# One kernel, three edits: the last head group's values computed features by tokens and mixed two units to a bank, two output tiles by halves, and products exchanged at both ends of the down product

## The chip, the cores and the metric

The kernel runs on one core of a Trainium2 chip. The metric is the device time of one launch in microseconds; of several launches the median is taken. The profile is that of one execution.

## What is computed

Two layers over x of 1024 tokens by 1024 features, in float32. Each layer does this (cut from the reference):

```
hn = rmsnorm(h, norm1[i]);  z = hn @ w_in[i]
u = z[..., :256];  q, k, v = split(z[..., 256:], 3)          # 12 heads of 64
pool_out = pool_mixer(u, pool_w[i], pool_scale[i])
attn_out = dilated_mixer(rotary(q), rotary(k), v)            # 3 groups of 4 heads: (128,1) (512,4) (2048,16)
h = h + concatenate([pool_out, attn_out]) @ w_out[i]
h = h + square(relu(rmsnorm(h, norm2[i]) @ w_up[i])) @ w_down[i]
gate = sigmoid(rmsnorm(h, norm3[i]) @ w_gate[i])
h = h + gate * (p[i] @ w_ple[i])
```

A group's output is weighted per token and head by a softmax over the three groups' denominators, which is known only when all three groups have their scores.

## The kernel before

Activations stand features by tokens, 128 features to a tile, 1024 tokens in two halves of 512. A float32 product is made of three fp32r matmuls (high by high, high by low, low by high); `split` makes the high part on ScalarE and the low part on VectorE. `Weights.next()` hands out a group of weight columns, waits on the program's clock until its high and low parts have been issued, and begins the next group 0.6 us later, with 0.9 us from one step to the next.

Nothing is scheduled by the compiler: instructions go out in the order in which the program issues them, engine by engine. That order comes from a clock `ck` of the program's own. `ck.tick(ns)` advances it for each matmul and runs the generators that have come due; a generator issues some instructions and yields the delay to its next step; `ck.need(key)` runs queued events, and moves the clock on to them, until the key has been issued; some helpers add to `ck.now` for the matmuls that they issue themselves. So delays in the code are a plan, not waits: on the chip, engines wait for each other by semaphores, in the order issued.

In a layer the input product runs group by group: q, k, v of the first two groups, q and k of the third, the two tiles `us` of the pooling columns, and last the third group's values. For those, hT is the stationary operand: eight tiles v2p of 128 tokens by 256 features, 24 matmuls of 256 columns each; ScalarE scales them by the norm into v2. As each tile is ready, `alone(u)` mixes one unit of 128 tokens: four small matmuls into bank o (eight records in the trace), two ScalarE copies into oT. In the same stretch the pooling mixer ends (`mixed`: py on VectorE from sums pa and pb on GpSimd, then two matmuls pm for each tile, L944, split by L536 and L538), `joint` makes the softmax weights (jt, jw, a round trip through DRAM, wb), and `weigh` multiplies o by wb (L1026) and splits it into cat (L532, L534). Pooling's second tile begins T_M1 = 13.0 us, on the program's clock, after the last pooling product.

The output product follows: for m in 0 to 5 one weight group, two halves po, evicted by `out_evac`; the last two tiles are done together.

Up and down products use seven products instead of eight per 2x2 block (P1 to P7, in the Strassen manner). `Set.open` gives P1, P6, P5 and P3 of a set one bank X, P2 a bank Y, P7 and P4 a bank Z. A bank is read out after each product (in the down product by VectorE into acc, L1294), and the next product of the same bank adds to what is there, so it waits until that read is done. `Seven` makes the weight pieces (d0p, d1p) ahead of the products by planned times; `D7.lead` starts its plan before the down product begins. `x_back` loads the pieces wP of the squared activations that `Up.sums` wrote to DRAM. For the last two up sets (`rush`) these sums wait 33 us.

PSUM has 8 banks: mm 3, s 2, e 2, o 1.

Of the kernel before, what the change touches and what calls it, by code (L numbers as in the profile page):

```python
# [117 lines left out]
def body(nc, tc, pools, A, out):  # L118
# [3 lines left out]
    def blk(name, dt=F32, shape=(128, 1024)):  # L122
        return sb.tile(list(shape), dt, name=name, tag="b")

    def bank(name, tag, shape=(128, 512)):
        return ps.tile(list(shape), F32, name=name, tag=tag)
# [4 lines left out]
    def hs(hf):  # L131
        return slice(hf * 512, hf * 512 + 512)
# [207 lines left out]
    for L in range(DEPTH):  # L340
        wi, wo, wu, wd, wg = (A[n][L] for n in ("w_in", "w_out", "w_up", "w_down", "w_gate"))
        g1 = G_N1 + 8 * L

        def col(part, g):
            return POOLW + 768 * part + 256 * g

        for g in range(NPAT):
            for part in range(2 if g == 2 else 3):
                for m in range(2):
                    groups.append([(wi, 0, 8, col(part, g) + 128 * m, 128, g1)])  # L350
        for m in range(2):
            groups.append([(wi, 0, 8, 128 * m, 128, g1)])
        groups.append([(wi, 4 * a, 4, col(2, 2), 256, g1) for a in range(2)])
        for m in range(8):
            groups.append([(wo, 0, 8, 128 * m, 128, None)])
        sevens.append(([(wu, 0, 4, 256 * j) for j in range(FF // 256)],
                       [(wd, a, n, 256 * t) for t, a, n in STEPS]))
        dn0.append(len(groups))
        for rep in range(2 if L == DEPTH - 1 else 1):
            for m in range(8):  # L360
                groups.append([(wg, 0, 8, m * 128, 128, None)])
            for m in range(2):
                pgroups.append([(A["w_ple"][L], 0, 2, m * 512, 512, None)])
# [177 lines left out]
    def pair(name):  # L541
        return blk(name + "H", F32R), blk(name + "L", F32R)
# [80 lines left out]
    def layer(L, hT, norm, tabs):  # L623
# [97 lines left out]
        vdone = set()  # L721

        def vok(g, n, p):
            return ((2, n) if g == 2 else (g, p, n // 4)) in vdone

        def in_v(g):
            vs = []
# [127 lines left out]
        def attend(g, q, k, vget, base, gap, late):  # L855

            o = [blk(f"o{g}{p}_{L}") for p in range(2)]
            oT[g] = o
            units = [Unit(g, n, q, k, vget, o) for n in range(8)]

            def alone(u):
                yield 1500.0
                while not vok(g, u.n, 0):
                    yield 500.0
                u.mix()

            def beats():
                t = ck.now
                for i in range(8 + 2 * late):
                    if 0 <= i - late < 8:  # L870
                        u = units[i - late]
                        u.turn()
                        if g == 2:
                            ck.go(alone(u))
                    if g < 2 and i >= 2 * late:
                        u = units[i - 2 * late]
                        while not (vok(g, u.n, 0) and vok(g, u.n, 1)):
                            yield 500.0
                        u.mix()
                    if i < 8:  # L880
                        units[i].scores()
                    t += gap
                    yield max(100.0, t - ck.now)
            ck.go(beats(), delay=base)

        for g in range(2):
            q = in_qk(f"q{g}", g)
# [3 lines left out]
                   5000.0, 5900.0, 1)  # L891
        q = in_qk("q2", 2)
        k = in_qk("k2", 2)
        v2 = [blk(f"v2{a}_{L}", F32, (128, 4, 256)) for a in range(2)]
        attend(2, q, k, lambda n, h: v2[n // 4][:, n % 4, 64 * h:64 * h + 64],
               3500.0, 2500.0, 2)


        us = [blk(f"u{m}_{L}") for m in range(2)]
# [143 lines left out]
        for i in range(4):  # L1043
            cat[2 + i] = pair(f"cat{2 + i}_{L}")
            for hf in range(2):
                ck.go(weigh(i // 2, i % 2, hf), (id(cat[2 + i][0]), hf), W_0 + W_1 * (2 * i + hf))
        for t in range(8):
            p = bank(f"v2p{L}", "mm", (128, 256))
            tc_ = slice(t * 128, t * 128 + 128)
            for kk in range(8):  # L1050
                h, l = hT[kk]
                wh, wl = (x[:, kk % 4] for x in w[kk // 4])
                nc.tensor.matmul(p, h[:, tc_], wh, start=kk == 0, stop=False)
                nc.tensor.matmul(p, l[:, tc_], wh, start=False, stop=False)
                nc.tensor.matmul(p, h[:, tc_], wl, start=False, stop=kk == 7)
                if kk < 7:
                    ck.tick(330.0)
            nc.scalar.activation(v2[t // 4][:, t % 4], p, AF.Copy, scale=norm.rt[:, t:t + 1])
            ck.at(600.0, lambda t=t: vdone.add((2, t)))
            ck.tick(330.0)  # L1060
            if t in (3, 7):
                for i in (4, 5):
                    if t == 3:
                        cat[2 + i] = pair(f"cat{2 + i}_{L}")
                    hf = t // 7
                    ck.go(weigh(2, i % 2, hf), (id(cat[2 + i][0]), hf), 2500.0 + 900.0 * (i - 4))


        norm2 = Norm(f"b{L}")
# [95 lines left out]
        S7 = Seven(sevens[L][0], seq, f"u{L}", side=4)  # L1165

        catl = [cat[i] for i in range(8)]
        for m in range(6):
            w = W.next()
            if m == 5:  # L1170
                W.begin(W.i + 1, delay=5000.0)
            for hf in range(2):
                p = bank(f"po{L}", "mm")
                products(p, wk(w, range(8)), catl, hs(hf))
                ck.go(out_evac(p, m, hf))
# [29 lines left out]
        class Up(Set):  # L1205
# [34 lines left out]
            def sums(self, y):  # L1240
# [5 lines left out]
                nc.sync.dma_start(out=d[:, 0], in_=y[:, :512])  # L1246
                rush = self.j >= n7 - 2
                if rush:
                    yield 33000.0
                sub = nc.vector.tensor_tensor  # L1250
                slow = 1500.0 if rush else 700.0
                b11, b12, b21, b22 = y[:, :512], y[:, 512:], self.y2[:, :512], self.y2[:, 512:]
# [59 lines left out]
        seq2 = [(0, P) for P in RING[:6]]  # L1312
        for k in range(1, nst - 2):
            seq2 += [(k, "P1"), (k - 1, "P3")] + [(k, P) for P in RING[1:6]]
        seq2 += [(nst - 3, "P3")]
        seq2 += [(k, P) for P in ORDER for k in (nst - 2, nst - 1)]
        D7 = Seven(sevens[L][1], seq2, f"d{L}", (9, 6, 3))

        def run(S, seq, qs, objs, xs_of):
# [3 lines left out]
            for (j, P), o in zip(seq[qs[0]:], outs):  # L1323
                objs[j].close(o[0], P)

        live = {j: Up(j) for j in range(n7)}
        run(S7, seq, range(4), live, lambda j: xs)
        run(S7, seq, range(4, 6), live, lambda j: xs)
        for q in range(6, len(seq)):
            run(S7, seq, [q], live, lambda j: xs)  # L1330
            if q == len(seq) - 5:
                acc_load(0)
            if q == len(seq) - 8:
                D7.lead(8 * 12 * 225.0)
            n = q - len(seq) + 15
            if n > 0 and n % 2 == 0:
                for i in range(4):
                    ck.at(1500.0 * i + 300.0 * n, lambda i=i, P=seq[q][1]: ck.go(x_back(i, P)))


        live = {k: Down(k) for k in range(nst)}
        for q, (k, P) in enumerate(seq2):
            t, a, n = STEPS[k]
            if P == "P4" and k < 3:
# [1 line left out]
            if P == "P1":  # L1346
                if k >= nst - 2 and norm3 is None:
                    norm3 = Norm(f"c{L}")
            run(D7, seq2, [q], live, lambda k: xw[a:a + n])
            if t % 2 and k < nst - 2:  # L1350
                ck.go(x_back(a + 4, P))
                ck.at(5000.0, lambda i=a + 5, P=P: ck.go(x_back(i, P)))
# [236 lines left out]
```

## Time and profile before

| | |
|---|---|
| median of 3 runs | 2268.42 us (2268.37 to 2268.53) |
| profiled execution | 2269.02 us, span 2267.2 us, mean granted TensorE clock 0.999 |
| TensorE matmuls | 2240.3 us busy, 99% of the span |
| VectorE, ScalarE, GpSimd | 72%, 45%, 14% |

A span runs from the first to the last instruction. Matmuls overlap in the records, so what one costs is read from start to start, not from its duration. An idle time is put to the engine and instruction whose end came last before the waiting instruction began.

### The profile page before, as it was taken

What the parts mean: (1) busy time and instruction counts of PE and PEld (TensorE: products, weight loads), DVE (VectorE), ACT (ScalarE), POOL (GpSimd) and SP (SyncE); (2) the same over time, 40 slices, a digit from 0 to 9 for tenths busy, and PEclk for the clock granted to TensorE, in tenths of its full rate; (3) what the DMA queues carried; (4) which work ended last, traced back from release to release, by engine and by line L of the source; (5) the groups of instructions that cost most, each with busy time, mean ns of one, the idle gap of its engine ahead of it and who ended that gap; (6) DMA issues with size and microseconds to landing.
All of it is one profiled execution on the core that took longest, in us unless ns stands there. A gap on an engine that the chain in (4) does not pass through costs nothing.

```text
span 2267.2 us, 30544 instructions
## 1 busy us (share of the span) xinstructions
PE 2240.3 (99%) x11088; PEld 1849.0 (82%) x11088; DVE 1643.2 (72%) x3046; ACT 1011.6 (45%) x2147; POOL 313.9 (14%) x282
## 2 busy tenths in 40 slices
PE   8999999999999999999999999999999999999998
PEld 6887788888887888878887878888888878888888
DVE  6565757877778888796565567687777798888845
ACT  6244533533335434364324355444333453434645
POOL 5121135100000000022121122330000000000322
PEclk9999999999999999999999999999999999999999
DMA  6011133354448745431220122234445675546224
GB/s 186 19 48 20 39 94 112 124 167 150 150 143 271 239 135 171 149 112 47 61 62 19 39 49 61 81 112 153 153 154 160 209 247 175 162 140 181 69 62 134
DMA packets 296367, 275.63 MB, mean 122 GB/s; under 512 B 12476, under 2 KB 224056, under 8 KB 296216
## 3 DMA queue, kind: packets, MB, share of 16 engines
q1 hardware_dynamic: 293624, 270.04, 38.6%
q0 software_dynamic: 2272, 3.61, 0.9%
q8 instruction: 87, 1.43, 0.3%
q14 instruction: 64, 0.52, 0.1%
q10 hardware_dynamic: 320, 0.03, 0.0%
HBM read 200.99 MB, written 72.58 MB: 121 GB/s over the span
## 4 chain that ended last, share of the span: by engine, by line
PE 91%; DVE 5%; DMA 1%; ACT 1%; issue 1%; POOL 1%; SPq 0%; DVEq 0%; ACTq 0%
PE X L567 29%; PE Z L567 14%; PE Y L567 7%; PE in L552 5%; PE in L554 5%; PE in L550 5%; PE gt L554 3%; PE gt L552 3%; PE gt L550 3%; PE po L552 2%; PE po L550 2%; PE po L578 2%; PE po L554 2%; PE o L836 2%; PE s L785 2%
## 5 line engine op out<-in xcount | busy, mean ns | idle before, releaser
L458 POOL TENSOR_TENSOR sq_c<-sq_c,sqt_c 128x512 f32<-128x512 f32 x28 | 41.8, 1496 | 1162.0 <-ACT sqt_c L456 1161.1
L567 PE MATMUL X<-wP,d0p 128*128 128x512 f32 x768 | 180.2, 390 | 3.2 <-DVE acc L1294 2.5
L567 PE MATMUL X<-wP,d1p 128*128 128x512 f32 x768 | 180.1, 390 | 3.2 <-DVE acc L1294 2.5
L567 PE MATMUL X<-xP,u1p 128*128 128x512 f32 x768 | 182.2, 389 | 0.0
L567 PE MATMUL X<-xP,u0p 128*128 128x512 f32 x768 | 182.2, 389 | 0.0
L567 PEld LDWEIGHTS X<-wP,d0p 128*128 128x128 f32 x768 | 143.8, 188 | 34.6 <-ACT wP L1275 2.0
L567 PEld LDWEIGHTS X<-wP,d1p 128*128 128x128 f32 x768 | 143.8, 188 | 34.6 <-ACT wP L1275 2.0
L1277 DVE TENSOR_TENSOR wP<-wP 128x512 fp32r<-128x512 f32 x252 | 171.0, 697 | 0.9 <-ACT wP L1275 0.9
L567 PEld LDWEIGHTS X<-xP,u1p 128*128 128x128 f32 x768 | 143.9, 188 | 29.8
L567 PEld LDWEIGHTS X<-xP,u0p 128*128 128x128 f32 x768 | 143.9, 188 | 29.8
L1235 ACT ACTIVATE y<-y 128x1024 f32<-128x1024 f32 x64 | 67.3, 1055 | 199.2 <-DVE y L1232 199.1
L191 DVE SCALAR_TENSOR_TENSOR wl<-wr,gt,wh 128x128 fp32r<-128x128 f32 (+1 forms) x288 | 117.8, 440 | 44.4 <-ACT wh L197 44.1
L1275 ACT ACTIVATE wP<-wP 128x512 fp32r<-128x512 f32 x252 | 146.7, 617 | 0.2
L1294 DVE TENSOR_TENSOR acc<-acc,X 128x512 f32<-128x512 f32 x128 | 87.4, 683 | 55.6 <-PE X L567 55.6
L804 ACT ACTIVATE sm<-sm,nm 128x128 f32<-128x128 f32 (+1 forms) x192 | 84.3, 440 | 79.9 <-DVE nm L801 77.6
L197 ACT ACTIVATE wh<-wr,gt 128x128 fp32r<-128x128 f32 (+1 forms) x304 | 101.8, 397 | 0.9 <-DMA wr<-in_w_in_dram 0.8
L680 POOL TENSOR_TENSOR rot<-rot,s 128x512 f32<-128x512 f32 x48 | 61.6, 1288 | 255.6 <-DVE rot L678 136.7
L567 PE MATMUL Z<-wP,d1p 128*128 128x512 f32 x384 | 92.1, 389 | 1.0 <-DVE acc L1294 1.0
L567 PE MATMUL Z<-wP,d0p 128*128 128x512 f32 x384 | 92.1, 389 | 1.0 <-DVE acc L1294 1.0
L567 PE MATMUL Z<-xP,u1p 128*128 128x512 f32 x384 | 91.6, 389 | 0.0
L567 PE MATMUL Z<-xP,u0p 128*128 128x512 f32 x384 | 91.6, 389 | 0.0
L567 PEld LDWEIGHTS Z<-wP,d0p 128*128 128x128 f32 x384 | 72.0, 188 | 16.4 <-DVE acc L1294 1.4
(474 smaller groups left out, 5510.1 us busy)
## 6 DMA issues: line engine op xcount, KB each, us to landing
wP<-x_d SPq DMA_DIRECT2D x252, 256.0 KB, 3.4
x_d<-ys SPq DMA_DIRECT2D x64, 512.0 KB, 3.7
wr<-in_w_in_dram SPq DMA_DIRECT2D x40, 512.0 KB, 4.2
u0r<-in_w_up_dram SPq DMA_DIRECT2D x32, 512.0 KB, 5.1
x_d<-y SPq DMA_DIRECT2D x32, 512.0 KB, 2.8
u1r<-in_w_up_dram SPq DMA_DIRECT2D x32, 512.0 KB, 5.4
d0r<-in_w_down_dram SPq DMA_DIRECT2D x28, 512.0 KB, 6.2
d1r<-in_w_down_dram SPq DMA_DIRECT2D x28, 512.0 KB, 5.9
```

Source lines behind the costliest of these rows:

```text
L191: nc.vector.scalar_tensor_tensor(l[:, k], raw[:, k], gs[k], f(h[:, k]), op0=OP.mult, op1=OP.subtract)
L197: nc.scalar.activation(h[:, k], raw[:, k], AF.Copy, scale=gs[k])
L550: nc.tensor.matmul(p, wh, h[:, cols], start=first and i == 0, stop=False)
L552: nc.tensor.matmul(p, wh, l[:, cols], start=False, stop=False)
L554: nc.tensor.matmul(p, wl, h[:, cols], start=False, stop=last and i == n - 1)
L567: nc.tensor.matmul(p, w[:, a, i], x[:, b], start=first and i == 0 and a == b == 0, stop=i == n - 1 and a == 1, skip_group_check=not first)
L680: nc.gpsimd.tensor_tensor(a, a, tb["s"][:, hs(hf)], op=OP.mult)
L804: nc.scalar.activation(self.sm[:, p, hh], self.sm[:, p, hh], AF.Exp, bias=nm[:, h:h + 1], scale=0.125, accum_out=ml[g][:, n, 4 + h:5 + h])
L1235: nc.scalar.activation(y, y, AF.Square)
L1275: nc.scalar.activation(t[:, 0], f(t[:, 1]), AF.Copy)
L1277: nc.vector.tensor_tensor(t[:, 1], f(t[:, 1]), f(t[:, 0]), op=OP.subtract)
L1294: nc.vector.tensor_tensor(a, a, p, op=OP.add)
```

## The change

The third group's values are made like those of the first two: two weight groups of 128 features, each the stationary operand for 512 tokens, evicted by VectorE with the norm into vt2. `mix_half` then transposes four blocks of each tile into a bank, copies them into v2, and mixes four units, two to a bank, with two wider copies each. Both weight groups are taken before the first product. The first two output tiles are done by halves: first half of both, then second half of both. In the down product, P1 of the first set goes ahead of the last up product, and at the end P3 of one set goes between the P1s of the last two sets. The last two up sets' sums wait 46 us instead of 33, and the lead is 7 products instead of 8.

```diff
-        groups.append([(wi, 4 * a, 4, col(2, 2), 256, g1) for a in range(2)])
+        for m in range(2):
+            groups.append([(wi, 0, 8, col(2, 2) + 128 * m, 128, g1)])
...
-            def alone(u):
-                yield 1500.0
-                while not vok(g, u.n, 0):
-                    yield 500.0
-                u.mix()
...
-        for t in range(8):
-            p = bank(f"v2p{L}", "mm", (128, 256))
...
-            nc.scalar.activation(v2[t // 4][:, t % 4], p, AF.Copy, scale=norm.rt[:, t:t + 1])
-            ck.at(600.0, lambda t=t: vdone.add((2, t)))
...
+        ws = [w, W.next()]
+        vts = []
+        for m in range(2):
+            vts.append(blk(f"vt2{m}_{L}"))
+            v2.append(blk(f"v2{m}_{L}", F32, (128, 8, 128)))
+        def mix_half(b):
+            yield 2200.0
+            for m in range(2):
+                p = bank(f"vp2_{L}", "e", (128, 4, 128))
+                for i in range(4):
+                    n = 4 * b + i
+                    nc.tensor.transpose(p[:, i], vts[m][:, n * 128:n * 128 + 128], ident)
+                ck.now += 430.0
+                nc.scalar.activation(v2[m][:, 4 * b:4 * b + 4], p, AF.Copy)
+            yield 2000.0
+            for c in range(2):
+                us_ = units2[4 * b + 2 * c:4 * b + 2 * c + 2]
+                op = bank(f"o2_{L}", "os"[c], (128, 2, 2, 128))
+                for i, u in enumerate(us_):
+                    for p, hh, h in u.heads:
+                        nc.tensor.matmul(op[64 * hh:64 * hh + 64, i, p], u.vget(u.n, h), u.et[:, p, hh, 0],
+                                         start=True, stop=True)
+                ck.now += 860.0
+                n = us_[0].n
+                for p in range(2):
+                    nc.scalar.activation(oT[2][p][:, n * 128:n * 128 + 256]
+                                         .rearrange("p (i c) -> p i c", i=2), op[:, :, p], AF.Copy)
+                for u in us_:
+                    ck.waiting.discard(("o", 2, u.n, 1))
+        for hf in range(2):
+            for m in range(2):
+                p = bank(f"in{L}", "mm")
+                products(p, wk(ws[m], range(8)), hT, hs(hf))
+                nc.vector.tensor_tensor(vts[m][:, hs(hf)], p, norm.bc[:, hs(hf)], op=OP.mult)
+            ck.go(mix_half(hf))
+            for i in (4, 5):
+                if hf == 0:
+                    cat[2 + i] = pair(f"cat{2 + i}_{L}")
+                ck.go(weigh(2, i % 2, hf), (id(cat[2 + i][0]), hf), 6500.0 + 900.0 * (i - 4))
...
-        for m in range(6):
+        w = W.next()
+        ws = [w, W.next()]
+        for hf in range(2):
+            for m in range(2):
+                p = bank(f"po{L}", "mm")
+                products(p, wk(ws[m], range(8)), catl, hs(hf))
+                ck.go(out_evac(p, m, hf))
+        ws = None
+        for m in range(2, 6):
...
-                    yield 33000.0
+                    yield 46000.0
...
-        seq2 += [(nst - 3, "P3")]
-        seq2 += [(k, P) for P in ORDER for k in (nst - 2, nst - 1)]
+        seq2 += [(nst - 2, "P1"), (nst - 3, "P3"), (nst - 1, "P1")]
+        seq2 += [(k, P) for P in ORDER[1:] for k in (nst - 2, nst - 1)]
...
         for q in range(6, len(seq)):
+            if q == len(seq) - 1:
+                run(D7, seq2, [0], downs, lambda k: xw[0:4])
             run(S7, seq, [q], live, lambda j: xs)
...
-                D7.lead(8 * 12 * 225.0)
+                D7.lead(7 * 12 * 225.0)
...
-            run(D7, seq2, [q], live, lambda k: xw[a:a + n])
+            if q:
+                run(D7, seq2, [q], live, lambda k: xw[a:a + n])
```

## Rows read from the trace of the kernel before

**Rows 1.** The page: TensorE's line of busy times, the chain by engine.
```profile
PE 2240.3 (99%) x11088; PEld 1849.0 (82%) x11088; DVE 1643.2 (72%) x3046; ACT 1011.6 (45%) x2147; POOL 313.9 (14%) x282
...
PE 91%; DVE 5%; DMA 1%; ACT 1%; issue 1%; POOL 1%; SPq 0%; DVEq 0%; ACTq 0%
```

**Rows 2.** TensorE's waits, whole span: us in total, times, longest.
```profile
PE X L567 <- DVE acc L1294: 5.0, 4, 1.6
...
PE Z L567 <- DVE acc L1294: 2.0, 2, 1.0
...
PE o L836 <- ACT v L1058: 0.6, 2, 0.3
```

**Rows 3.** Timeline of VectorE, 676 to 725 us: start, us, what.
```profile
715.64 0.68 DVE L1294 TENSOR_TENSOR acc<-acc,X 128x512 f32<-128x512 f32 x1
...
719.25 0.68 DVE L1294 TENSOR_TENSOR acc<-acc,Z 128x512 f32<-128x512 f32 x1
```

**Rows 4.** Timeline of VectorE, 736 to 790 us.
```profile
745.21 0.68 DVE L1254 TENSOR_TENSOR ys<-y,y 128x512 f32<-128x512 f32 x1
...
760.56 0.68 DVE L1294 TENSOR_TENSOR acc<-acc,Z 128x512 f32<-128x512 f32 x1
```

**Rows 5.** Windows, the values in both layers: PE, PEld, DVE, ACT, POOL, PEclk.
```profile
281.46:313.71 32.25, 31.97 (x259) 27.85 (x257) 22.79 (x42) 14.26 (x35) 11.88 (x11) 1.00 0.46 117
1393.38:1425.63 32.25, 31.97 (x259) 27.85 (x257) 22.74 (x42) 14.26 (x35) 11.89 (x11) 1.00 0.46 117
```

**Rows 6.** Timeline of TensorE, 281 to 289 us, first layer.
```profile
281.46 0.28 PE L1053 MATMUL v2p<-wh,h_0H 128*128 128x256 f32 x1
...
281.81 1.02 PE L944 MATMUL pm<-py,pw 128*128 128x512 f32 x2
...
282.78 0.28 PE L1054 MATMUL v2p<-wh,h_1L 128*128 128x256 f32 x1
...
284.34 0.28 PE L1055 MATMUL v2p<-wl,h_5H 128*128 128x256 f32 x1
...
286.62 0.28 PE L1055 MATMUL v2p<-wl,h_1H 128*128 128x256 f32 x1
286.83 0.66 PE L836 MATMUL o<-et,v 128*64 128x128 f32 x8
...
287.64 0.28 PE L1054 MATMUL v2p<-wh,h_2L 128*128 128x256 f32 x1
...
288.95 0.27 PE L982 MATMUL jt<-cst,jt 128*96 128x128 f32 x1
```

**Rows 7.** The same timeline, 276 to 279 us.
```profile
276.57 0.39 PE L552 MATMUL in<-h_2L,wh 128*128 128x512 f32 x1
...
278.42 0.39 PE L550 MATMUL in<-h_5H,wh 128*128 128x512 f32 x1
```

**Rows 8.** Timeline of TensorE in an earlier group, 91 to 119 us.
```profile
92.24 0.60 PE L742 MATMUL vp<-cst,vt 128*128 128x128 f32 x4
...
92.90 0.39 PE L554 MATMUL in<-h_3H,wl 128*128 128x512 f32 x1
...
116.94 1.15 PE L836 MATMUL o<-et,v 128*64 128x128 f32 x16
```

**Rows 9.** Timeline of GpSimd, 268 to 330 us.
```profile
292.48 0.19 POOL L911 COPY pa<-pb 128x4 f32<-128x4 f32 x1
```

**Rows 10.** Timeline of VectorE, 278 to 330 us.
```profile
284.62 0.74 DVE L538 SCALAR_TENSOR_TENSOR cat_0L<-pm,gt,cat_0H 128x512 fp32r<-128x512 f32 x1
...
292.70 3.00 DVE L931 SCALAR_TENSOR_TENSOR py<-pa,cst,u 64x1024 f32<-64x1024 f32 x1 [3.16 <-POOL pa L911]
...
297.62 2.54 DVE L1026 TENSOR_TENSOR o<-o,wb 128x512 f32<-128x512 f32 x4
```

**Rows 11.** Windows at the end of the span: as rows 5.
```profile
2260.00:2261.00 1.00, 0.04 (x1) 0.00 (x0) 0.66 (x4) 0.19 (x1) 0.00 (x0) 1.00 0.00 0
...
2262.00:2263.00 1.00, 0.00 (x0) 0.00 (x0) 0.70 (x2) 0.61 (x1) 0.00 (x0) 0.50 0.11 43
```

More of the change, by code (lines that the diff above doesn't have):

```diff
@@ L723, in vok @@
         def vok(g, n, p):
-            return ((2, n) if g == 2 else (g, p, n // 4)) in vdone
+            return (g, p, n // 4) in vdone
         def in_v(g):
@@ L872, in beats @@
                         u.turn()
-                        if g == 2:
-                            ck.go(alone(u))
                     if g < 2 and i >= 2 * late:
@@ L884, in attend @@
             ck.go(beats(), delay=base)
+            return units
         for g in range(2):
@@ L893, in layer @@
         k = in_qk("k2", 2)
-        v2 = [blk(f"v2{a}_{L}", F32, (128, 4, 256)) for a in range(2)]
-        attend(2, q, k, lambda n, h: v2[n // 4][:, n % 4, 64 * h:64 * h + 64],
-               3500.0, 2500.0, 2)
+        v2 = []
+        units2 = attend(2, q, k, lambda n, h: v2[h // 2][:, n, 64 * (h % 2):64 * (h % 2) + 64],
+                        3500.0, 2500.0, 2)
         us = [blk(f"u{m}_{L}") for m in range(2)]
@@ L1046, in layer @@
                 ck.go(weigh(i // 2, i % 2, hf), (id(cat[2 + i][0]), hf), W_0 + W_1 * (2 * i + hf))
-        for t in range(8):
-            p = bank(f"v2p{L}", "mm", (128, 256))
[L1049 to L1057, printed above, removed]
-            nc.scalar.activation(v2[t // 4][:, t % 4], p, AF.Copy, scale=norm.rt[:, t:t + 1])
-            ck.at(600.0, lambda t=t: vdone.add((2, t)))
[L1060 to L1066, printed above, removed]
+        ws = [w, W.next()]
@@ L1167, in layer @@
         catl = [cat[i] for i in range(8)]
-        for m in range(6):
+        w = W.next()
[5 more added lines that the diff above has]
+                ck.go(out_evac(p, m, hf))
+        ws = None
+        for m in range(2, 6):
             w = W.next()
@@ L1324, in run @@
                 objs[j].close(o[0], P)
+        downs = {k: Down(k) for k in range(nst)}
         live = {j: Up(j) for j in range(n7)}
@@ L1338, in layer @@
                     ck.at(1500.0 * i + 300.0 * n, lambda i=i, P=seq[q][1]: ck.go(x_back(i, P)))
-        live = {k: Down(k) for k in range(nst)}
+        live = downs
         for q, (k, P) in enumerate(seq2):
```

## Prediction

> **What bounds the kernel now.** I read the page first. TensorE has a matmul running 99% of the span, and the chain that ended last lies on it for 91% [rows 1]. So time changes in two ways only: TensorE gets other instructions, or it waits more or less. Its whole list of waits is short; beyond the first 30 us the largest are 5.0 us in four waits and 2.0 us in two, all for VectorE's additions into acc in the down product [rows 2]. That is 7.0 us in both layers, and it is all that the exchanges can give directly.
>
> The exchange at the front of the down product aims at the wait at 716 us. VectorE adds product P1 of the first set only at 715.64 us [rows 3], and P6, two products later, goes into the same bank. With the last up product between them, TensorE has 12 more matmuls to do in the meantime. The 13 us longer delay aims at the second wait: from 745.21 us on the last two sets' sums stand in VectorE's queue, and the addition that Z needs runs at 760.56 us [rows 4]. The exchange at the back separates P5 and P3 of one set, which share a bank. Both layers show the same pair of waits [rows 2].
>
> **The values, work alone.** The stage takes 32.25 us in each layer [rows 5]. Its terms [rows 6]: a 256-column matmul comes every 0.12 us (13 from 282.78 to 284.34), so 192 are 23.0 us. A unit of mixing costs 287.64 - 286.62 - 0.24 = 0.78 us, a pair of pooling matmuls 282.78 - 281.46 - 4 x 0.12 = 0.84 us. With seven units, four pairs and one wait of 0.3 us [rows 2] that is 32.2 us, so nothing is missing; the eighth unit runs inside the output product, 33.0 us in all.
>
> After: 96 matmuls of 512 columns. In the input product eight took 278.42 - 276.57 = 1.85 us, 0.231 each [rows 7], so 22.2 us. Sixteen transposes are new: four cost 92.90 - 92.24 - 0.23 = 0.43 us [rows 8], so 1.7 us. Four units now stand in a row; 16 mixing records took 1.15 us where 8 took 0.66 [rows 6, 8], so a unit more costs 0.49 us, four are 0.78 + 3 x 0.49 = 2.25 us, eight 4.5 us. Pooling stays 3.4 us. Sum 31.8 us: 1.2 us less per layer (between 0.8 and 1.6 with 0.004 us either way for the input matmul).
>
> The Trainium skill (TensorE: Matmul & The Clock Gate, "Back-to-back issue gap") gives N/2.4 + 2.5 ns, that is 109 and 216 ns; by it the products save 0.2 us instead of 0.8, and the rows here, 120 and 231 ns, decide. The same page ("Part 4: PE-mode transpose") reports some 275 ns for a transpose in a kernel; if that were the spacing, sixteen would be 4.4 us and the change would lose 1.5 us per layer by work alone, but the row has four in 0.43 us.
>
> **The values, order.** This is what decides. Each engine's order comes from the program's clock ck, which moves only by ticks of issued matmuls, or by jumping when need() must run queued events. I call T the clock at the first matmul of the values (281.46 us in the first layer). Before, W.next() is called once there. Now it is called twice in a row. The first call begins the second tile's weights at T + 0.6 with eight steps of 0.9; the second call needs them finished. No matmul is issued between, so the clock jumps to about T + 8.4 (7.8, and 0.6 for two pooling pairs' own 0.86 advances). Everything due in that time is issued ahead of the first value product, and everything due later stands 8 us of TensorE's work too early.
>
> That the program's clock sets the order exactly can be tested on before: pooling's first pair is due within T + 0.33 and stands after three matmuls; mixing's first unit after two k steps of the second tile, jt's transpose four k steps later, as the ticks of 0.33 give [rows 6].
>
> In the new order the clock has the first product's eviction at T + 13.6, just behind the first half of py (T_M1 = 13.0), the second's at T + 18.7, pooling's third pair at T + 19, and transposes at T + 20.9. Ahead of the second eviction VectorE's queue holds both halves of py, the first eviction, four multiplications of o by wb (T + 15), their four low parts (T + 16.5) and two more multiplications (T + 17.7). VectorE runs in that order, and it can't run early: py waits for GpSimd's pa until 292.67 us [rows 9] and ends at 297.6, when the multiplications begin [rows 10].
>
> TensorE by contrast gets there early. Two pooling pairs: 283.1. Then jt's transpose needs the first pair's bank, which L538 gave back at 285.36 [rows 10]; a short scaling of weights replaces a longer operation ahead of it, so I take 284.6, **1.5 us of waiting** (0 to 2.3). Products of the first half: 48 x 0.231 = 11.1 us, to 295.8. Pooling's third pair then waits for py, 297.6 + 0.68 for the eviction within it = 298.3: **2.3 us** after one or two matmuls (1.6 to 3). Pair, some six matmuls and the first four transposes: 301.0. The other four need the second eviction: 298.3 + 4 x 0.635 + 4 x 0.63 + 2 x 0.63 + 0.68 = 305.3 (multiplication from the row of four in 2.54 us [rows 10], a low part taken as equal, an eviction as the 0.68 of the same shape [rows 3]): **4.3 us** (3 to 7, the upper end if the bank of the pooling pair is the last to come free). Two small ones remain: the next pooling pair's bank, and the second half's eviction at the start of the output product, where its two W.next() jump 2.8 us past the transposes: 0.5 us together (0 to 1.5). Sum 8.6 us, less 1.2 of work: 7.4 us per layer.
>
> TensorE's granted clock adds something. It reads 1.00 all through this stage [rows 5]; the fall that I see comes after the last matmul: 1.00 to 2261, 0.50 from 2262 us, 2 us later [rows 11]. A wait of 4.3 us reaches that far. No row shows the return; at 1.2 GHz a matmul of 0.231 us would take twice that. Between 0 and 2 us per layer I take 1.0, a few such matmuls. Both layers: 2 x 8.4 = +16.8 us.
>
> What follows is covered: the pieces of cat for the second half are now first needed after two products instead of one (24 x 0.23 = 5.5 us later), and that is what hides mix_half(1) and its eight mixing units, ACT copies and weighing. Without that cover it would cost those 5.5 us. The eight ACT copies of o saved bring nothing: ACT is busy 14.3 of 32.25 us here [rows 5].
>
> **The exchanges, cost.** P1's weights and the four x pieces are needed 2.7 us earlier; D7.lead with 7 for 8 starts them 2.7 us earlier too, so cover stays the same. VectorE's queue is full there, and P4 into Z needs the addition that ran at 719.25 [rows 3], to 719.93; without the wait P4 starts near 720.1. So the first wait goes nearly whole, 1.6 us, with 0 to 0.5 given back. The sums, moved past 758 us, leave 0 to 1.0 of the second wait; I take it gone. At the back the rest goes, (7.0 - 3.2 - 2.0) / 2 = 0.9 us, but the pieces that VectorE makes for the last sets behind it do not move with it: 0.5 given back (0 to 0.9). That is 3.0 us per layer (2 to 3.7), **-6.0 us** in all.
>
> **Sum.** The profiled execution took 2269.02 us for a span of 2267.2, 0.6 over the median 2268.42. It becomes 2269.0 + 16.8 - 6.0 = 2279.8; against the median **2279.2**, I say 2279.
>
> **Rivals.**
> First, the jump does no harm (another side: faster). If VectorE's evictions came without the queue ahead of them, only work and exchanges count: 2268.4 - 2.4 - 6.0 = 2260 (2257 to 2264). For it: VectorE is busy only 22.8 of 32.25 us [rows 5]. Against it: those idle times are waits for GpSimd and ScalarE in a queue that stays in order. It decides if the second eviction stands ahead of the four multiplications.
> Second, part of the queue is ahead: py alone delays TensorE (1.5 + 2.3 us), the transposes don't. Then 2 x (3.8 - 1.2) - 6.0 = -0.8: 2267.6, no change (2264 to 2272).
> Third, the stalls as forecast, and the exchange doesn't do what it says, since VectorE's full queue only moves the wait on: 2285. It is the upper part of my case.
>
> **Chances.** Forecast with the third rival 0.64, its own range 2273 to 2287; the harmless jump 0.27; the half-way case 0.09. What a measurement here can tell from no change is about 0.2%, 4.5 us: 2263.9 to 2272.9. Faster 0.28, same 0.07, slower 0.65. The range runs from 2258 to 2286, which leaves out some 0.1 at either end.
>
> **What would show it.** Right: TensorE's waits list vp2 <- VectorE vt2 with 4 us or more in each layer, pm <- py about 2 us, and jt <- L538; the stage up to the output product's first matmul grows from 32.25 us to some 37; X and Z <- acc shrink from 7.0 us to below 2. Wrong: no wait for vt2, or the evictions ahead of o <- o,wb on VectorE; then it is the first rival. Acc waits that stay at 7 us would make the exchange's step wrong. Wrong in size: if the clock is at 0.50 for much of the stage, or if mixing or the output product waits for cat, which I count as covered.

## The result: 2304.19 us, slower, and above the range

| | before | after |
|---|---|---|
| median | 2268.39 us (2268.23 to 2268.53, 4 runs) | 2304.19 us (2303.59 to 2304.9, 4 runs) |
| profiled execution | 2269.02 us, span 2267.2 | 2304.25 us, span 2302.5 |

The ratio is 1.0158, 95% interval 1.0142 to 1.0173: slower, as forecast, by 35.8 us instead of 10.8. On the page of the kernel after, TensorE (PE) is still the bound. Its matmul records grew by 11.8 us against [rows 1], although there are 160 records fewer: at half clock each is longer, as the windows below show.

```profile
PE 2252.1 (98%) x10928; PEld 1848.6 (80%) x10928; DVE 1662.4 (72%) x3070; ACT 1011.1 (44%) x2139; POOL 310.5 (13%) x282
...
PE 89%; DVE 5%; DMA 2%; issue 1%; ACT 1%; SPq 0%; POOL 0%; DVEq 0%; ACTq 0%
```

Where the time went is read from TensorE's timeline, from the first matmul of one stage to the first of the next:

| stage | before, layers 0 and 1 | after | difference |
|---|---|---|---|
| input product, values | 303.5, 292.7 | 314.6, 304.1 | +11.1, +11.4 |
| output product | 87.9, 87.9 | 89.3, 89.3 | +1.4, +1.4 |
| up and down products | 617.9, 617.9 | 623.4, 622.9 | +5.5, +5.0 |
| gate and rest | 113.4, 135.8 | 113.4, 135.8 | 0, 0 |

TensorE's list of waits names most of it (us in total, times, longest); it answers to [rows 2].

```profile
PE vp L1054 <- ACT v L1056: 12.8, 2, 6.6
PE X L568 <- DVE acc L1319: 8.1, 4, 3.6
...
PE pm L938 <- DVE py L933: 4.4, 2, 2.2
PE vp L1054 <- DVE vt L1077: 1.6, 2, 0.8
...
PE pm L938 <- ACT v L1056: 1.4, 2, 0.7
...
PE jt L976 <- DVE cat_0L L539: 1.0, 1, 1.0
```

Each wait that the prediction gave the values is there: jt 1.0 us (layer 1's has the same), pm on py 2.2, the output's start 0.8. The largest, 6.4 us per layer, stands at the transposes, but the list names ScalarE's copy v and not VectorE's eviction vt. In the down product the waits on acc did not shrink from 7.0 us, they stand at 8.1. The stage of the values, up to the output product's first matmul, took 44.2 us (280.06 to 324.23) where I had some 37.

**The values of layer 0.** TensorE's timeline (start, duration, the idle time before in brackets with what ended it):

```profile
280.06 1.88 PE L938 MATMUL pm<-py,pw 128*128 128x512 f32 x4
282.94 0.31 PE L976 MATMUL jt<-cst,jt 128*96 128x128 f32 x1 [1.00 <-DVE cat_0L L539]
...
297.03 1.13 PE L938 MATMUL pm<-py,pw 128*128 128x512 f32 x2 [2.18 <-DVE py L933]
...
298.91 0.60 PE L1054 MATMUL vp<-cst,vt 128*128 128x128 f32 x4
305.73 1.11 PE L1054 MATMUL vp<-cst,vt 128*128 128x128 f32 x4 [6.23 <-ACT v L1056]
307.54 2.07 PE L938 MATMUL pm<-py,pw 128*128 128x512 f32 x2 [0.69 <-ACT v L1056]
...
323.81 0.66 PE L1054 MATMUL vp<-cst,vt 128*128 128x128 f32 x4 [0.79 <-DVE vt L1077]
324.23 0.48 PE L551 MATMUL po<-cat_0H,wh 128*128 128x512 f32 x1
```

The two pooling pairs stand together ahead of the first value product, and py, four multiplications and four low parts stand on VectorE between the evictions, as the clock's jump says:

```profile
294.71 0.68 DVE L1077 TENSOR_TENSOR vt<-in,rs_a 128x512 f32<-128x512 f32 x1
...
296.80 0.17 DVE L933 TENSOR_TENSOR py<-pt,u 64x16 f32<-64x16 f32 x1
297.01 2.74 DVE L1020 TENSOR_TENSOR o<-o,wb 128x512 f32<-128x512 f32 x4
299.66 2.49 DVE L535 TENSOR_TENSOR cat_0L<-o,cat_0H 128x512 fp32r<-128x512 f32 x4
302.07 0.69 DVE L1077 TENSOR_TENSOR vt<-in,rs_a 128x512 f32<-128x512 f32 x1
```

The second eviction ends at 302.76 us, and the transposes that need it begin 3 us later. ScalarE's timeline shows what they wait for: `mix_half` takes one bank of the two e for each four transposes, and the bank comes free when ScalarE has copied an earlier four. The other e bank is held by the pooling pair of 297.03 us, which VectorE reads last at 311.04 us (cat_0L from pm). ScalarE's copy stands behind the pieces of cat:

```profile
298.63 1.77 ACT L533 ACTIVATE cat_0H<-o 128x512 fp32r<-128x512 f32 x3 [0.27 <-DVE o L1020]
303.39 1.23 ACT L533 ACTIVATE cat_0H<-o 128x512 fp32r<-128x512 f32 x2 [2.98 <-DVE o L1020]
304.52 0.67 ACT L537 ACTIVATE cat_0H<-pm,gt 128x512 fp32r<-128x512 f32 x1
305.09 0.59 ACT L1056 ACTIVATE v<-vp 128x512 f32<-128x512 f32 x1
```

TensorE's first four blocks were ready at 299.5 us; the copy ran at 305.09, because ScalarE waited 2.98 us in order for two multiplications that VectorE did after the eviction. So the chain goes through VectorE, the whole queue ahead of the eviction and more, and once through ScalarE.

**TensorE's clock.** The windows show what such a wait does after itself (PEclk, the granted clock, is the third number from the end; 0.50 is 1.2 GHz):

```profile
302.00:303.00 1.00, 0.00 (x0) 0.00 (x0) 1.00 (x3) 0.00 (x0) 0.00 (x0) 0.81 0.91 246
303.00:304.00 1.00, 0.00 (x0) 0.00 (x0) 0.95 (x2) 0.61 (x2) 0.00 (x0) 0.50 0.21 57
...
311.00:312.00 1.00, 1.00 (x3) 0.35 (x2) 0.96 (x2) 0.00 (x0) 0.00 (x0) 0.50 0.00 0
312.00:313.00 1.00, 1.00 (x11) 0.90 (x12) 1.00 (x3) 0.00 (x0) 0.00 (x0) 0.57 0.00 0
313.00:314.00 1.00, 1.00 (x22) 1.00 (x20) 0.66 (x1) 0.84 (x2) 0.00 (x0) 1.00 0.00 0
```

TensorE idles from 299.5 us; the granted clock is 0.50 from 303 on and returns near 312.9, 7 us after the matmuls went on at 305.73. In between the value product's matmuls come every 0.43 us instead of 0.23.

**The down product of layer 0.** The first wait of [rows 3] is gone. A new one stands where before had none, at 784.82 us, with twelve matmuls in 5.26 us behind it (2.72 at full clock):

```profile
784.82 5.46 PE L568 MATMUL X<-wP,d0p 128*128 128x512 f32 x12 [3.63 <-DVE acc L1319]
790.08 3.21 PE L568 MATMUL Z<-wP,d0p 128*128 128x512 f32 x12
```

VectorE's addition for it runs at 784.00 us. Back in VectorE's queue stands a wait of 3.67 us, and on ScalarE one of 9.11:

```profile
779.18 0.69 DVE L333 TENSOR_TENSOR d0p<-d0s,d0p 128x512 fp32r<-128x512 f32 x1 [3.67 <-ACT d0p L331]
...
784.00 0.68 DVE L1319 TENSOR_TENSOR acc<-acc,X 128x512 f32<-128x512 f32 x1
```

```profile
778.51 0.63 ACT L331 ACTIVATE d0p<-d0s 128x512 fp32r<-128x512 f32 x1 [9.11 <-PE X L568]
```

ScalarE's instruction makes the high part of a weight sum d0s. It reads nothing of TensorE's. That it waits for a product of bank X can only be for the place that it writes: `blk` hands out SBUF buffers of one common pool (tag "b"), in the program's order, and the next one to come back is the piece that this product reads. So the reading is: too few buffers, one engine stands for 9 us, and two engines behind it. Who took the buffers is what the experiments ask.

### The profile page after: what moved, and what is told of

It reads as the page before. It is cut to its first block, busy times and chain, and to the rows that moved or that the text cites. A ratio compares the mean times of both kernels' runs of the same rounds, so it can differ in the third digit from the quotient of the medians.

```text
span 2302.5 us, 30241 instructions
## 1 busy us (share of the span) xinstructions
PE 2252.1 (98%) x10928; PEld 1848.6 (80%) x10928; DVE 1662.4 (72%) x3070; ACT 1011.1 (44%) x2139; POOL 310.5 (13%) x282
## 4 chain that ended last, share of the span: by engine, by line
PE 89%; DVE 5%; DMA 2%; issue 1%; ACT 1%; SPq 0%; POOL 0%; DVEq 0%; ACTq 0%
PE X L568 28%; PE Z L568 14%; PE Y L568 7%; PE in L553 6%; PE in L555 6%; PE in L551 5%; PE gt L553 3%; PE gt L555 3%; PE gt L551 3%; PE po L553 2%; PE po L551 2%; PE po L555 2%; PE po L579 2%; PE s L786 2%; PE o L837 1%
## 5 line engine op out<-in xcount | busy, mean ns | idle before, releaser
L191 DVE SCALAR_TENSOR_TENSOR wl<-wr,gt,wh 128x128 fp32r<-128x128 f32 x304 | 131.5, 465 | 44.4 <-ACT wh L197 43.9
L197 ACT ACTIVATE wh<-wr,gt 128x128 fp32r<-128x128 f32 x320 | 105.4, 391 | 0.6 <-DMA wr<-in_w_in_dram 0.5
L568 PEld LDWEIGHTS Z<-wP,d1p 128*128 128x128 f32 x384 | 72.2, 189 | 16.7 <-DVE wP L1302 1.7
```

What stands on the lines that cost most here:

```text
L191: nc.vector.scalar_tensor_tensor(l[:, k], raw[:, k], gs[k], f(h[:, k]), op0=OP.mult, op1=OP.subtract)
L197: nc.scalar.activation(h[:, k], raw[:, k], AF.Copy, scale=gs[k])
L568: nc.tensor.matmul(p, w[:, a, i], x[:, b], start=first and i == 0 and a == b == 0, stop=i == n - 1 and a == 1, skip_group_check=not first)
```

## The experiments

Theory **O** (order): the clock's jump at the values, by the two `W.next()`, costs 12 us per layer. Theory **B** (buffers): the sums moved from 33 to 46 us keep their tiles y and ys while the last loads of acc take two more buffers for good, and ScalarE's weight pieces run out of room. Rivals: the exchanges cause the new wait; or the time is VectorE's and ScalarE's longer queue.

**Parts alone.** `vals_only` is the kernel before with the values and the output halves alone. Against the kernel after (P1 of the first set stands behind the last up product again, with a lead of 8):

```diff
-                    yield 46000.0
+                    yield 33000.0
...
-        seq2 += [(nst - 2, "P1"), (nst - 3, "P3"), (nst - 1, "P1")]
+        seq2 += [(nst - 3, "P3")]
```

> The kernel before with the values and the two output tiles changed, the down product as before. Theory (the jump of the program's clock makes TensorE wait): all 12 us per layer that the input and output stages grew by in the changed kernel stay, so 2268.4 + 2 x 12.4 = 2293 us, with the same waits for py and vt2. Rival (the loss of the changed kernel comes from its down product, which disturbs the next layer as well): below 2280 us.

Measured 2292.81 us, ratio 1.0108 (1.0093 to 1.0123). The waits are those of the change: vp on v 12.9 us, pm on py 4.4, and acc as before, 5.0 and 2.0. So the values cost 24.4 us, whatever the rest does.

`exchange_only` is the kernel before with both exchanges and the lead of 7, sums at 33 us.

> The kernel before with P1 ahead of the last up product, P3 between the last P1s and the lead of 7, sums still at 33 us. Theory (the exchanges are good, the later sums are what harms): the waits of 1.6 and 0.9 us per layer go, 2268.4 - 5 = 2263 us. Rival (an exchange itself makes the down product of the changed kernel 5 us longer per layer): 2278 us or so.

Measured 2267.51 us, 0.9996 (0.9987 to 1.0006): nothing that can be told from no change, a miss. The acc waits did fall, from 7.0 to 1.8 us; X on ScalarE's wP 1.1, Z on VectorE's wP 1.0, X on VectorE's wP 0.4 came up.

`rush46_only` is the kernel before with one number changed:

```diff
-                    yield 33000.0
+                    yield 46000.0
```

> The kernel before with the last two up sets' sums at 46 instead of 33 us, nothing else. Theory (four y buffers are held 13 us longer, so a weight piece waits for a buffer, and VectorE and TensorE behind it): the wait of 1.0 us near 760 us goes, one of some 3.6 us near 780 us comes, with matmuls at the lower clock behind it, 2 x 5 = 10 us more: 2278 us. Rival (what the prediction said, the sums are better off later): 2266 us.

Measured 2278.52 us, 1.0045 (1.0029 to 1.0062). The second wait on acc (Z, 2.0 us) is gone, as forecast, and a larger one has come. In TensorE's list and on ScalarE:

```profile
PE X L567 <- DVE acc L1294: 5.0, 4, 1.6
...
PE X L567 <- ACT d0p L331: 4.2, 1, 4.2
PE X L567 <- ACT d1p L331: 4.2, 1, 4.2
```

```profile
765.35 0.63 ACT L331 ACTIVATE d0p<-d0s 128x512 fp32r<-128x512 f32 x1 [9.11 <-PE X L567]
```

It is the same 9.11 us without any exchange, so the exchanges don't cause it. The kernel before has such waits too, the longest of them 4.8 us between 700 and 800 us, and TensorE has no wait for a weight piece in that stretch. Two later weight pieces on ScalarE, which read nothing of the moved sums ys, begin 0.03 and 0.04 us after an operation on ys has ended, and TensorE's wait of 4.23 us (to 772.26 us) is put down to the second:

```profile
768.54 0.63 ACT L331 ACTIVATE d0p<-d0s 128x512 fp32r<-128x512 f32 x1 [0.68 <-DVE ys L1256]
771.55 0.63 ACT L331 ACTIVATE d0p<-d0r 128x512 fp32r<-128x512 f32 x1 [2.38 <-DVE ys L1258]
```

(`rush40_only` is this kernel once more, despite its label: 2279.29 us, one run.)

`after_rush33` is the kernel after with 33 us.

> The changed kernel with the sums back at 33 us. Theory: the 3.6 us wait and the lower clock near 780 us go, in both layers: 2304.2 - 2 x 6.6 = 2291 us, or a little less, the down product no longer than before. Rival (the exchange at the front makes that wait): still 2300 us or more.

Measured 2292.92 us, 1.0108: the 46 us cost 11.3 us there too, and acc falls to 1.7 us in all. The three parts measured alone add up to 24.4 - 0.9 + 10.1 = 33.6 of the 35.8 us.

**Is it the jump?** `early_weights_33` takes the jump away and leaves the work: the second value weight group is begun during the last pooling product, so that `W.next()` finds it finished.

```diff
-        def in_tile(evac):
+        def in_tile(evac, more=None):
             w = W.next()
+            if more is not None:
+                W.begin(W.i + 1, delay=more)
...
-            in_tile(u_evac)
+            in_tile(u_evac, 2500.0 if m else None)
...
-                    yield 46000.0
+                    yield 33000.0
```

> The changed kernel with sums at 33 us, and the second group of value weights begun during the last pooling product, so that the second W.next() finds it ready and the program's clock does not jump. Theory (the jump makes the waits): the waits for py, vt2, the copy of v2 and jt go, the input stages shrink by some 11 us per layer, and the work saved shows: 2268.4 - 2.4 (values) - 0.8 (exchanges) = 2265 us. Rival (VectorE's queue is too full for features-by-tokens values in any order): waits of several us for vt2 remain, 2280 us or more.

Measured 2268.40 us, 1.0002 (0.9993 to 1.001), 24.5 us below `after_rush33` and some 3 above the expected 2265. The waits of jt, of pm, and of vp on v are gone; left is vp on vt, 2.5 us, at the output product, whose weights jump as well. With 46 us (`early_weights_46`):

> The same with the sums at 46 us, the changed kernel's own. Theory (the two losses are independent): 2265 + 11.3 (what 46 us cost in the changed kernel) = 2276 us. Rival (the late down stage comes of the late input stage): within 2 us of the run with 33 us.

Measured 2276.94 us, 1.0039 (1.0025 to 1.0053): without the jump the 46 us still cost 8.5 us. `early_both` begins the output's second group early too (sums at 33 us):

```diff
         ws = [w, W.next()]
+        W.begin(W.i + 1, delay=9000.0)
```

> The changed kernel with sums at 33 us, the second value weights begun during the last pooling product, and the second output weights begun during the values, so that neither pair of W.next() makes the clock jump. Theory: the last wait for vt2 (1.3 us per layer) goes as well, and the work saved shows: 2268.4 - 2.6 = 2265.8 us. Rival (the waits for weights or buffers only move): 2268 us or more.

Measured 2265.60 us, 0.9988 (0.9979 to 0.9996). TensorE's timeline has the pooling pairs apart again and the eight transposes in one run, with no idle time before any of them:

```profile
281.61 1.02 PE L940 MATMUL pm<-py,pw 128*128 128x512 f32 x2
283.86 1.02 PE L940 MATMUL pm<-py,pw 128*128 128x512 f32 x2
...
296.67 1.03 PE L1057 MATMUL vp<-cst,vt 128*128 128x128 f32 x8
299.93 1.97 PE L1066 MATMUL o<-et,v 128*64 128x128 f32 x32
```

`values_early_both` is that without the exchanges, the values' work alone.

> The same without the exchanges: the kernel before with the values and output tiles changed and both second weight groups begun early. Theory: input and output stages 1.2 us shorter per layer, 2268.4 - 2.4 = 2266.0 us. Rival (no gain without a full pool's cost elsewhere): 2268.4 us.

Measured 2266.67 us, 0.9992 (0.9983 to 1.0001): 1.8 us below before by the medians, which by themselves the interval doesn't tell from nothing.

**Is it buffers?** `hold_two` is the kernel before with two buffers held longer: one y of each of the last two up sets is read once more.

```diff
+                if rush:
+                    s = None
+                    t = small.tile([128, 2], F32, name="held", bufs=1, tag="held")
+                    yield 3300.0
+                    nc.vector.tensor_copy(t[:, 0:1], y[:, :1])
```

> The kernel before, with the sums where they were (33 us), but one of the two y buffers of each of the last two up sets read once more, by a copy of 128x1 on VectorE, 13 us after its last use: two buffers are held longer in each layer, and nothing else is moved. Theory (46 us cost buffers): a weight piece on ScalarE waits for a buffer and TensorE behind it, half or more of what rush46_only lost: 2272 to 2278 us. Rival (the sums' new place in VectorE's queue is what costs): 2268.5 us.

Measured 2268.54 us, 1.0000 (0.9991 to 1.001), with the waits of before. A miss: two buffers aren't enough to run out. `keep_six` leaves the sums at 33 us and takes six buffers after them for 13 us, with almost no work (one column each):

```diff
+                if self.j == n7 - 1:
+                    s = y = b11 = b12 = b21 = b22 = None
+                    self.y1 = self.y2 = None
+                    kept = [blk("kept") for _ in range(6)]
+                    for t in kept:
+                        nc.vector.memset(t[:, :1], 0.0)
+                    yield 13000.000000
+                    o = small.tile([128, 8], F32, name="held", bufs=1, tag="held")
+                    for i, t in enumerate(kept):
+                        nc.vector.tensor_copy(o[:, i:i + 1], t[:, :1])
```

> The kernel before, sums at 33 us; after them six more buffers of the same pool are taken, marked by six writes of 128x1 on VectorE, and read and given back 13 us later, so some 757 to 770 us: buffers are short there as with the later sums, and no sum is moved. Theory (46 us cost buffers): a weight piece on ScalarE waits several us for a buffer, VectorE's additions and TensorE behind it, 2270 to 2282 us. Rival (only the sums' place in VectorE's queue matters): 2268.5 us, the twelve small operations hidden.

Measured 2277.10 us, 1.0038 (1.0024 to 1.0052), and the wait on ScalarE is there to 0.01 us, though no sum moved; TensorE's waits for X on acc grow from 5.0 to 10.5 us, the longest of them 2.7 instead of 1.6:

```profile
768.05 0.63 ACT L331 ACTIVATE d0p<-d0s 128x512 fp32r<-128x512 f32 x1 [9.12 <-PE X L567]
```

`rush_40us` asks whether the price grows with the delay, as a queue's would, or has a threshold:

```diff
-                    yield 33000.0
+                    yield 40000.0
```

> The kernel before with the last two up sets' sums 40 us late instead of 33, nothing else. If what is lost at 46 us is a shortage of SBUF buffers (the sums' tiles meet the last loads of acc), the loss has a threshold: at 40 us the sums' tiles are given back 6 us before they are at 46, and either the wait of ScalarE's d0p for a buffer is there whole (2274 to 2279) or not at all (2266 to 2269). If the cost were more work or a longer queue, it would grow with the delay, and 40 us would give about half of it, 2273.

Measured 2268.77 us, 1.0000 (0.9991 to 1.001): at 40 us nothing is lost, 6 us later 10. A price that grows with the delay would have shown some half of the 10; a threshold, which theory B expects, is what the runs show. Nothing is gained either: Z's 2.0 us are gone from the list, and X's waits have grown by 2.5.

```profile
PE X L567 <- DVE acc L1294: 7.5, 6, 1.6
```

**Where did the exchanges' gain go?** `back_only` is the exchange at the back alone.

> The kernel before with the exchange at the back alone (P3 between the last two P1s). Theory (the wait is moved on: VectorE is full behind it): 0.9 us of waiting per layer goes and 0.5 to 0.9 comes back at d0p and acc within 30 us: 2267.5 us. Rival (the prediction's full gain): 2266.5 us.

Measured 2267.05 us, 0.9994 (0.9985 to 1.0003); acc falls from 7.0 to 6.2 us. `front_only` is the one at the front, with the lead of 7:

```diff
+        downs = {k: Down(k) for k in range(nst)}
...
+            if q == len(seq) - 1:
+                run(D7, seq2, [0], downs, lambda k: xw[0:4])
             run(S7, seq, [q], live, lambda j: xs)
...
-                D7.lead(8 * 12 * 225.0)
+                D7.lead(7 * 12 * 225.0)
```

> The kernel before with the exchange at the front of the down product and the shorter lead alone. By my forecast the first wait, 1.6 us per layer, goes with 0 to 0.5 given back: 2265.2 to 2266.2 us. Rival, the pieces take over: the first product of the down product starts one product earlier, and the x pieces wP that VectorE and ScalarE make end as late as before, so that TensorE waits for them instead of for acc: about 2268.4, with Z <- wP and X <- wP of 1 to 2 us in sum per layer where acc shrinks by 1.6 per layer.

Measured 2269.55 us, 1.0005 (0.9996 to 1.0013). The acc waits fell from 7.0 to 2.5 us, and the matmuls behind the exchange now wait for x pieces, those of P4 (bank Z) and of P3 (bank X):

```profile
722.19 0.96 PE L567 MATMUL Z<-wP,d0p 128*128 128x512 f32 x3 [0.24 <-DVE wP L1277]
...
732.52 0.50 PE L567 MATMUL X<-wP,d0p 128*128 128x512 f32 x1 [0.89 <-ACT wP L1275]
```

`front_early_x` starts just these earlier: n runs over the even numbers from 2 to 14, one for each of P1, P7, P6, P2, P5, P4 and P3, and only for 12 and 14 (P4 and P3) does the edit take the delay of 300 n away, 3.6 and 4.2 us. What the expectations of this run and of `both_and_early_x` say of the edit, and of its size, is wrong:

```diff
-                    ck.at(1500.0 * i + 300.0 * n, lambda i=i, P=seq[q][1]: ck.go(x_back(i, P)))
+                    ck.at(1500.0 * i + (300.0 * n if n < 12 else 0.0), lambda i=i, P=seq[q][1]: ck.go(x_back(i, P)))
```

> The same with the x pieces of the first twelve blocks of a product begun at once instead of 0.3 us apart, so that they stand up to 3.6 us earlier in the queues. If late x pieces are what gives the front exchange's gain back, the waits for wP shrink and the time is 1 to 2 us below that of the front exchange alone, 2266 to 2267. If VectorE's and ScalarE's full queues are the limit, an earlier place for these pieces only makes the others late, and the time is that of the front exchange alone or above it.

Measured 2266.11 us, 0.9989 (0.998 to 0.9998). Every wait for wP has left the list. Of the down product's waits it holds the additions, and the 0.7 us in each layer for weight pieces that before had too. Z's is P4 of the first set, 0.92 us, and the 0.4 that is left of the second wait:

```profile
PE Z L567 <- DVE acc L1294: 2.7, 4, 0.9
PE X L567 <- DVE acc L1294: 1.7, 2, 0.9
```

So the exchange does what it says once the pieces come with it: 1.2 us per layer in the stage of up and down products (616.7 us against 617.9 in layer 0; `front_only` 618.4).

**Both causes mended.** `both_and_early_x` is `early_both` with the x pieces of `front_early_x`.

> The changed kernel with the sums back at 33 us, the second weight groups of the values and of the output begun early, and the x pieces of five products of the last up products begun 0.6 to 3.0 us earlier. If the two causes add up, 2265.6 less the 2.5 that the earlier x pieces gave between 2269.55 and 2266.11 (and at most 3.4): 2262 to 2263.5. Rival: the exchange at the back already fills the queues, and the earlier pieces only move the wait on: 2265 to 2266.

Measured 2262.57 us, ratio 0.9974 (0.9964 to 0.9984): faster than before by 5.8 us and than after by 41.6, with no wait left for wP, py, jt or vt.

```profile
PE Z L568 <- DVE acc L1322: 2.7, 4, 0.9
...
PE X L568 <- DVE acc L1322: 0.9, 2, 0.5
```

## Why the prediction was right in sign and wrong in size

**The step that failed: "The exchanges, cost".** It gave the exchanges and the later sums together -6.0 us; alone they measured +10.1 (the sums) and -0.9 (the exchanges), and the stage grew by 5.5 and 5.0 us. It failed in two places.

"The sums, moved past 758 us, leave 0 to 1.0 of the second wait; I take it gone." The wait is gone, in `rush46_only` as forecast. What I didn't cost is what the sums hold while they wait. I looked for what the move does to VectorE's queue and not at the pool of buffers; `keep_six` shows that buffers alone give the same wait on ScalarE and cost 8.6 us, where the later sums cost 10.1, and `rush_40us` that the price has a threshold between 40 and 46 us. The price is the wait of TensorE, 3.6 us in the kernel after, 4.2 in `rush46_only`, and the half clock behind it, 5.26 + 3.05 - 2 x 2.72 = 2.9 us for the two products that begin at 784.82 and 790.08 us. The place of the sums has a part in the wait: four of their operations, 0.6 us each, stand on VectorE between its own wait and the addition at 784.00 us, and in `keep_six`, where none does, TensorE waits 2.74 us. No run separates the two exactly. That the sums' tiles hold places which weight pieces wait for is borne out by the two late pieces in `rush46_only`; that the loads of acc help to fill the pool I read from the code, and no run changed the loads.

"D7.lead with 7 for 8 starts them 2.7 us earlier too, so cover stays the same." That holds for the weight pieces. The four x pieces are issued by `x_back`, at fixed delays after the up products, and D7.lead does not move them. `front_only` shows the waits for wP that follow, and `front_early_x`, which moves only the pieces of P4 and P3, takes them away. With the pieces moved the exchange brings 1.2 us per layer: 1.63 of the first wait less the 0.92 that P4 then waits for Z, and 0.6 of the second wait. I had 1.1 to 1.6 from the first wait alone, since by my working P4 would start when its addition is done; so the first wait's term was about 0.7. At the back, 0.4 net was forecast per layer and 0.7 measured, too little to tell.

**The order of the values: the mechanism right, its terms mis-sized.** Without the jump, 24.5 us come back (`early_weights_33`), so the first two rivals, for which VectorE's queue would have had to let the evictions through, are out. Per layer, forecast and measured: jt 1.5 and 1.0; pm on py 2.3 and 2.2; the last transposes 4.3 and 6.4; the two small ones 0.5 and 0.7 + 0.8; work -1.2, and -0.9 from `values_early_both` (half of 1.8). The transposes are part of that work: eight in 1.03 us in `early_both`, so the price of the row of four held. The Trainium skill (TensorE: Matmul & The Clock Gate, "Part 4: PE-mode transpose") has some 275 ns for one in a kernel; taken as the spacing that would be, as an estimate, 2.2 us for eight, and this trace shows less than half of it. The waits and the work give 10.2; the stages grew by 12.5 to 12.8, so about 2.5 us is left for the clock, where I had 1.0. The second eviction came at 302.07 us, 2.5 us earlier than the 304.6 that I worked out, because the multiplications had started earlier (297.01), and four stood ahead of it and not six. And yet TensorE waited longer, for it too came earlier (299.5 us instead of 301.0), and the transposes began at 305.73. That this is close to the forecast 305.3 is luck, since what it waited for was not that eviction: I followed VectorE's queue alone, and named the bank only as the upper end, and that of the pooling pair. It was the bank of the transposes themselves, freed by a ScalarE copy behind pieces of cat that wait for VectorE. So the wait of 6.4 us lies in the estimate's range of 3 to 7 by another path than the one that gave the 4.3.

**The clock.** I took it as a few matmuls at half rate because no row showed the return. The rows above show it: 7 us at 0.50 after one wait of 6.2 us, 6 us after one of 3.6. Counted with it, the wait of 3.63 us cost 6.5 in the kernel after, and that of 6.2 some 8.7. This is no fixed price: in `early_weights_46` the same wait of 3.63 us had only 1.4 us of half clock behind it (twelve matmuls in 4.16 us instead of 2.72), which over two layers makes up the difference between the 11.3 us that the later sums cost in the kernel after and the 8.5 here.

**The third rival**, that the exchange only moves the wait on (2285 us), came nearest in place: it is right for the exchanges alone. With the order's true size it would have given 2268.4 + 24.4 - 0.9 = 2291.9, and `after_rush33` measured 2292.92. The 11.3 us beyond that are the sums' buffers, and that case stood among my rivals nowhere; a "moved later" was costed at its queue and not at what it keeps occupied.

**What stays open.** 2.2 of the 35.8 us appear only with the parts together. The parts' intervals of some 3 us each hold that, and the profiled executions show where it can come from: behind the wait at the sums the half clock cost 2.9 us in the kernel after and 1.7 in `rush46_only` (twelve matmuls in 4.40 us), in each of two layers. How many buffers are short is not known: two, held where `hold_two` holds them, were not enough to show, and six where `keep_six` takes them were.

## What to carry to other kernels

When a step is moved later, list what it holds until then (buffers, banks) beside the queues that it leaves; an instruction that waits for an engine whose data it does not read may be waiting for a place to write, as ScalarE's pieces did here, and the wait spreads through every engine that runs in order behind it. When a product is moved earlier, move every operand's maker, and look up which of them the shift in the plan really reaches. Where a program's own clock jumps, make the thing that it waits for early instead of accepting the order behind the jump: here that was a line or two per place, and it took back the 24 us of loss; of the 2.4 us that the work alone promised, 1.8 were measured, at the edge of what the interval can tell.

## What the runs showed of the hardware that I had not expected

In the kernel after, the granted clock stayed at 1.00 for some 3 us of idle TensorE (from 299.5 to about 302.6, and from 781.2 to about 783.9) and was then 0.50 until 7.1 and 5.9 us after the next matmul. The length of a wait alone does not say what follows it. These rows, with the wait in brackets, are from `early_weights_46`, `keep_six` (both layers) and `after_rush33` (layer 1, with the windows behind it):

```profile
771.65 4.32 PE L568 MATMUL X<-wP,d0p 128*128 128x512 f32 x12 [3.63 <-DVE acc L1321]
```

```profile
772.11 3.00 PE L567 MATMUL X<-wP,d0p 128*128 128x512 f32 x12 [2.74 <-DVE acc L1304]
...
1887.03 4.57 PE L567 MATMUL X<-wP,d1p 128*128 128x512 f32 x12 [2.74 <-DVE acc L1304]
```

```profile
1421.69 1.66 PE L938 MATMUL pm<-py,pw 128*128 128x512 f32 x2 [2.19 <-DVE py L933]
```

```profile
1422.00:1423.00 1.00, 1.00 (x3) 0.34 (x1) 1.00 (x3) 0.61 (x1) 0.00 (x0) 0.57 0.98 229
1423.00:1424.00 1.00, 1.00 (x3) 0.67 (x2) 1.00 (x2) 0.97 (x3) 0.00 (x0) 0.50 1.09 254
```

Behind the same wait of 2.74 us the clock stayed at 1.00 in layer 0 (twelve matmuls in 2.84 us) and fell to 0.50 in layer 1 (4.41 us). Behind the wait of 2.2 us for py it stayed at 1.00 in both layers of the kernel after, and fell to 0.50 in layer 1 of `after_rush33`, at about 1422.1 us, when the matmuls had already gone on.

The wait for a place to write had the same length to 0.01 us in three kernels, 9.11, 9.11 and 9.12 us, although six other buffers had taken the sums' part in the third.
